# Seven block products for eight in the gate and up projections of a streaming encoder step on one Trainium2 core

## The chip, the cores and the metric

The kernel runs on one core of a Trainium2 chip. A core has a matrix engine (TensorE, in profiles PE, with its weight loads as PEld), a vector engine (DVE), an activation engine (ACT), a general engine (POOL, also GpSimd) and a queue engine (SP) that here issues the loads and stores. Tiles lie in SBUF on up to 128 partitions; matrix products accumulate in the banks of a second memory, PSUM. The metric is the device time of one execution in microseconds. Before the change it is 2217.21 us, the median of three runs from 2211.37 to 2221.53.

## The reference

One layer of a streaming encoder is applied to 1024 prompt frames and to 32 sample frames, with D_MODEL = 1024 and D_FF = 2816, all in fp32:

```python
def adaln_in(x, g, shift, scale):
    return rmsnorm(x, g) * (1 + scale[:, None, :]) + shift[:, None, :]

def swiglu(h, w_gate, w_up, w_down):
    return (jax.nn.silu(h @ w_gate) * (h @ w_up)) @ w_down

    mod = jax.nn.silu(c) @ w_mod + b_mod
    sh1, sc1, g1, sh2, sc2, g2, sh3, sc3, g3 = jnp.split(mod, N_MOD, axis=-1)
    h = adaln_in(x, gains[0], sh1, sc1)
    x = x + FFN_RES * g1[:, None] * rmsnorm(swiglu(h, w1_gate, w1_up, w1_down), gains[1])
    ...  # attention in two head groups, out-projection, residual with g2
    h = adaln_in(x, gains[4], sh3, sc3)
    x = x + FFN_RES * g3[:, None] * rmsnorm(swiglu(h, w2_gate, w2_up, w2_down), gains[5])
```

So two feed-forward networks (FFNs) stand around an attention part. The modulation is the product of SiLU(c) with a 1024 x 9216 matrix, for two vectors c (prompt and sample). The outputs are the new frames and the newest rows of keys and values.

## The kernel before

Activations lie transposed, features on partitions and tokens along the free dimension, in three token blocks: block 0 and block 1 of 384 tokens, block 2 of 288 (256 prompt frames and the 32 sample frames). A normed input `h` of a block is kept as two fp32r tiles, `h_hi` (the rounded value) and `h_lo` (the rest). A weight is loaded as fp32 (`raw`) and split in the same way: ACT copies it rounded into `w[:, 0]`, and DVE subtracts that from the raw tile into `w[:, 1]` (`split_w`, L299 to L305). A product of one 128-row k-tile is then three matmuls, high by high, high by low and low by high (`mm3`, L324 to L327).

An FFN (`ffn`, L525 on) goes over 11 groups of two hidden tiles of 128 columns. For each block and hidden tile, `up` makes the gate and the up product over 8 k-tiles in two PSUM banks, ACT applies SiLU, DVE multiplies, and the result is split into `gg`. `down` multiplies two hidden tiles into the 8 output tiles, two at a time in a two-bank tile `dn`, and DVE adds that to the accumulator `facc` (L581). The downs of a block are put one `up` behind (`late`). `rounds` gives the order of groups and blocks: in the first FFN ("h1") all blocks together, but the last three groups first for blocks 0 and 1 and then for block 2, and in the second ("h3") the first two groups for blocks 0 and 1 and then for block 2.

Other work runs beside the FFN as generators in the list `side`: `step(n)` takes n yields from the first of them. An `up` takes two steps after each of its two products (`PACE`), ten in the first group (`FAST`), and `down` one for each `dn`. In the first FFN these are the norms of the next blocks, and after the first group the modulation's remaining columns (`mod_aside`, L215 to L242: 14 chunks of 512 columns, made on DVE by multiplying raw rows with a per-partition scalar and adding, then transposed and reduced), and then the bias rows of attention. The first four chunks of the modulation are made on PE before the FFN starts (`mod_chunk`, L175), in the order of `START`. `need(key)` runs the side work until a key is done, `finish` until nothing is left. `between` makes a block's residual and its next norm; `finale` makes the output.

The order on each engine is chosen by a planner at build time: of the instructions that are ready by its own clock it takes the one that comes first in the program, and a tile is given a buffer when one of its pool is free. Pools live for the whole kernel: `wpool` (8 split weights), `rpool` (3 raw tiles), `gpool`, `hpool` (5 buffers) and `spool`; `upool` holds the large activation tiles. PSUM has two double banks (`p2`), three single ones (`p1`) and one more (`pc`). All loads go through SP's queue, in order.

## Time and profile before

| | |
|---|---|
| median of three runs | 2217.21 us (2211.37 to 2221.53) |
| profiled execution: span from first to last instruction | 2215.8 us; the page gives no other time for this execution |
| mean granted TensorE clock | 0.984 of full speed |
| busy PE, DVE, ACT, POOL | 2161.6, 1239.1, 697.8, 179.2 us |
| PE waits, longest in total | first input load 7.8 us; DVE's `ry` 4.8 us; POOL's `sq` 4.0 us |
| read from HBM, written | 164.12 MB, 22.86 MB |

A row of a group of instructions gives the line of the kernel, the engine and the operation, output and inputs by their names with partitions and elements, and the count; then the busy time and the mean of one in ns; then the idle time of the engine just before them and what ended it. A row of the timeline gives start, duration and the instruction. Matmuls overlap: the next starts before the one before it has ended, so the distance between two starts is the price of one, and the mean of one is not. A row of windows gives a stretch, its length, the busy time of PE, weight loads, DVE, ACT and POOL with the number of instructions, the granted clock, the DMA engines' share and GB/s; where only one tile is asked for, engines that do not touch it are left out.

### The profile page before, as it was taken

The page shows a single profiled execution, that of the slowest core. Times are in us where ns is not written, and L with a number is a line of the kernel's source. Part 1 is how long each engine was busy: PE and PEld are TensorE (multiplying, and loading weights), DVE is VectorE, ACT ScalarE, POOL GpSimd, SP SyncE. Part 2 cuts the span into 40 slices and gives each one's busy share as a digit, 9 for nine tenths or more (in the row PEclk, how much of TensorE's full clock was granted, in tenths as well). Part 3 has the DMA queues.
Part 4 walks back from the last instruction along what each step waited for, and adds up shares of the span by engine and source line. Part 5 has one row for each costly group of instructions (what it writes and reads, how often), then busy time and mean ns, then how long its engine had stood idle before and what let it go on. Part 6 is the DMA issues. An engine that isn't in the chain of part 4 may idle for free.

```text
span 2215.8 us, 33976 instructions
## 1 busy us (share of the span) xinstructions
PE 2161.6 (98%) x14012; PEld 2068.6 (93%) x14012; DVE 1239.1 (56%) x2425; ACT 697.8 (31%) x1450; POOL 179.2 (8%) x281
## 2 busy tenths in 40 slices
PE   6999999999999999899999899999999999999998
PEld 4999999999999999799787589999999999999998
DVE  5788667874333497677444865785333333333336
ACT  4411111111121253576444663542111111111133
POOL 1100000000000023001110313220000000000000
PEclk8999999999999999899999899999999999999999
DMA  9253334434122352111112121424211111111122
GB/s 323 93 153 118 111 96 124 143 101 129 39 66 69 101 184 93 38 39 30 50 30 62 46 77 67 134 86 120 66 58 39 57 39 39 58 38 58 39 69 79
DMA packets 200623, 186.03 MB, mean 84 GB/s; under 512 B 7597, under 2 KB 169813, under 8 KB 199317
## 3 DMA queue, kind: packets, MB, share of 16 engines
q1 hardware_dynamic: 200468, 183.87, 27.1%
q8 instruction: 110, 1.80, 0.3%
q14 instruction: 45, 0.36, 0.1%
HBM read 164.12 MB, written 22.86 MB: 84 GB/s over the span
## 4 chain that ended last, share of the span: by engine, by line
PE 90%; DVE 4%; DMA 3%; ACT 1%; issue 1%; POOL 0%; SPq 0%; ACTq 0%; DVEq 0%; POOLq 0%
PE dn L325 7%; PE dn L326 7%; PE dn L327 7%; PE gate L327 7%; PE gate L326 7%; PE up L327 7%; PE up L326 7%; PE gate L325 7%; PE up L325 7%; PE po L713 3%; PE S L752 2%; PE pq L325 2%; PE pq L327 2%; PE pq L326 2%; DMA raw<-in_w_gate_dram 1%; PE pp L776 1%
## 5 line engine op out<-in xcount | busy, mean ns | idle before, releaser
L326 PE MATMUL gate<-h_lo,w 128*128 128x384 f32 (+1 forms) x1056 | 340.2, 322 | 4.0 <-DVE h_lo L446 4.0
L325 PE MATMUL dn<-gg,w 128*128 128x384 f32 (+1 forms) x1056 | 341.4, 325 | 1.1 <-DVE facc L581 1.0
L581 DVE TENSOR_TENSOR facc<-dn,facc 128x768 f32<-128x768 f32 (+1 forms) x240 | 212.9, 889 | 230.2 <-PE dn L327 229.9
L326 PE MATMUL dn<-gg,w 128*128 128x384 f32 (+1 forms) x1056 | 340.6, 323 | 0.6 <-DVE gg L554 0.6
L325 PE MATMUL gate<-h_hi,w 128*128 128x384 f32 (+1 forms) x1056 | 341.0, 323 | 0.0
L327 PE MATMUL gate<-h_hi,w 128*128 128x384 f32 (+1 forms) x1056 | 340.4, 322 | 0.0
L325 PE MATMUL up<-h_hi,w 128*128 128x384 f32 (+1 forms) x1056 | 340.2, 322 | 0.0
L326 PE MATMUL up<-h_lo,w 128*128 128x384 f32 (+1 forms) x1056 | 340.0, 322 | 0.0
L327 PE MATMUL dn<-gg,w 128*128 128x384 f32 (+1 forms) x1056 | 340.0, 322 | 0.0
L327 PE MATMUL up<-h_hi,w 128*128 128x384 f32 (+1 forms) x1056 | 339.9, 322 | 0.0
L304 DVE TENSOR_TENSOR w<-raw,w 128x1024 fp32r<-128x1024 f32 x187 | 231.5, 1246 | 150.5 <-ACT w L303 150.3
L303 ACT ACTIVATE w<-raw 128x1024 fp32r<-128x1024 f32 x187 | 195.7, 1056 | 266.1 <-PE dn L327 103.5
L550 ACT ACTIVATE sl<-gate 128x384 f32<-128x384 f32 (+1 forms) x132 | 60.9, 462 | 563.9 <-PE gate L327 560.9
L551 DVE TENSOR_TENSOR sl<-sl,up 128x384 f32<-128x384 f32 (+1 forms) x132 | 68.5, 519 | 292.1 <-PE up L327 286.1
L326 PEld LDWEIGHTS gate<-h_lo,w 128*128 128x128 f32 x1056 | 198.6, 188 | 4.6 <-DVE h_lo L446 4.6
L325 PEld LDWEIGHTS dn<-gg,w 128*128 128x128 f32 x1056 | 199.2, 189 | 1.6 <-DVE facc L581 1.2
L326 PEld LDWEIGHTS dn<-gg,w 128*128 128x128 f32 x1056 | 199.2, 189 | 1.0 <-DVE gg L554 0.9
L327 PEld LDWEIGHTS dn<-gg,w 128*128 128x128 f32 x1056 | 199.1, 189 | 0.0
L325 PEld LDWEIGHTS gate<-h_hi,w 128*128 128x128 f32 x1056 | 198.7, 188 | 0.1
L327 PEld LDWEIGHTS gate<-h_hi,w 128*128 128x128 f32 x1056 | 198.7, 188 | 0.0
L327 PEld LDWEIGHTS up<-h_hi,w 128*128 128x128 f32 x1056 | 198.7, 188 | 0.0
L325 PEld LDWEIGHTS up<-h_hi,w 128*128 128x128 f32 x1056 | 198.5, 188 | 0.0
(224 smaller groups left out, 3367.4 us busy)
## 6 DMA issues: line engine op xcount, KB each, us to landing
raw<-in_w_mod_dram SPq DMA_DIRECT2D x56, 512.0 KB, 4.0
raw<-in_w_gate_dram SPq DMA_DIRECT2D x54, 512.0 KB, 4.0
raw<-in_w_up_dram SPq DMA_DIRECT2D x54, 512.0 KB, 4.7
raw<-in_w_down_dram SPq DMA_DIRECT2D x54, 512.0 KB, 4.5
raw<-in_w_in_dram SPq DMA_DIRECT2D x18, 512.0 KB, 4.3
wm<-in_w_mod_dram SPq DMA_DIRECT2D x8, 1024.0 KB, 7.4
raw<-in_w_out_dram SPq DMA_DIRECT2D x13, 512.0 KB, 4.5
xr<-xs SPq DMA_DIRECT2D x16, 384.0 KB, 3.5
```

Of the source, the lines that this page charges most:

```text
L303: ae.activation(w[:, 0], r, AF.Copy)
L304: ve.tensor_sub(w[:, 1], r, w[:, 0])
L325: te.matmul(ps, w[:, 0, k], hi, start=start, stop=False)
L326: te.matmul(ps, w[:, 0, k], lo, start=False, stop=False)
L327: te.matmul(ps, w[:, 1, k], hi, start=False, stop=stop)
L550: ae.activation(sl[:, :w], ps[0][:, :w], AF.Silu)
L551: ve.tensor_tensor(sl[:, :w], sl[:, :w], ps[1][:, :w], op=OP.mult)
L581: ve.tensor_tensor(o, ps[:, :, :w], o, op=OP.add)
L713: te.matmul(po[64 * h:64 * h + 64, :n], vsl(j, h, kn), PT(h, j, kn), start=j == 0, stop=j == nt - 1)
L752: te.matmul(S[:, c:ce], self.T[:, h, :], KQ[:, 0, 128 * k0 + c:128 * k0 + ce], start=True, stop=True)
L776: te.transpose(pp[:, j - j0, :], P[:, 128 * j:128 * j + 128], ident)
```

## The change

For each group, the gate and the up matrix are taken as 2 x 2 blocks: two hidden tiles (f) by two halves of the 1024 features (d), A11, A12, A21, A22, each four k-tiles of 128 columns. The inputs of blocks 0 and 1 are the 2 x 2 blocks on the other side: B11 and B21 are the halves of block 0, B12 and B22 those of block 1. Seven products (the Winograd form of Strassen's scheme) take the place of eight. Four weight sums S1 to S4 are made on POOL from raw quarters for each matrix of a group and then split like the other quarters; four input combinations T1 to T4 are made once per FFN (`combos`) from `h_hi + h_lo`, with half of the sums of high and low on POOL, and split again. The products are accumulated in PSUM where two follow on one another in the same bank (S2 and S3 in b, S1 and S4 in d, A11 and A12 in a), and DVE adds banks to SBUF tiles ("plus", five times a stage). Block 2 is multiplied by the plain quarters A11, A12, A22, A21 within the same stage. The first group of each FFN, and rounds that have only block 2, remain plain (`plain`), by quarters.

Gate, up and down of a group are now stages one after another, each for all its blocks; in a down stage the blocks come in the order 1, 0, 2. A stage's raw weights are loaded at the start of the stage before it, and its first sums or splits are made before that one ends (`ready`). A raw tile holds half of the features by two hidden tiles (1 KB rows) in place of all of them by one (512 B rows); the bytes are the same. Split weights are quarter tiles of 512 elements. `step(PACE)` is taken after each product of a Strassen stage, eight to a stage, or seven without block 2.

The modulation beside the FFN takes 384 columns at a time in 19 chunks, its raw rows in `hpool`, and yields ten times in a chunk, where it yielded 15 times. The pools of raw tiles, split weights, `gg` and small tiles, and a new one of large tiles `ux`, are opened anew for each of the three phases (`open_pools`), in the same addresses; an instruction on a new tile waits for the tiles that lay there before. At the start a modulation chunk is loaded by three transfers in place of two, and both hidden tiles' gate weights of the first group are loaded where the first hidden tile's gate and up were.

The core of the diff:

```diff
-ROUNDS = {"h1": ((), 3), "h3": ((((0, 1), 2), ((2,), 2)), 0)}
+ROUNDS = {"h1": (0, 3), "h3": (2, 0)}
+FFN1 = {"ux": 3, "r": 4, "w": 4, "g": 6, "s": 11}
+FFN2 = {"ux": 3, "r": 5, "w": 4, "g": 6, "s": 9}
+MIX = {"w": 8, "r": 3, "g": 5, "s": 5, "m": 1}
+MODS = [(("ux", 6), ("r", 2))] * 4
+SUMS_POOL = ("S1", "S2", "S3", "S4")
+ZPOOL = (1, 0, 1, 0)
+LATE = 1
...
+    def open_pools(name, **sizes):
+
+        phase.close()
+        pools.clear()
+        for tag, bufs in sizes.items():
+            pools[tag] = phase.enter_context(tc.tile_pool(name=name + tag, bufs=bufs, reuse_waits="tile"))
...
+    def mod_aside(c0, nc_):
+
+        w = 128 * nc_
+        acc = [s_tile([128, 384], "macc")[:, :w] for _ in range(2)]
         for g in range(4):
-            r = rpool.tile([128, 2, 512], F32, name="raw", tag="r")
-            dma.dma_start(r, w_mod[0, 256 * g:256 * (g + 1), 512 * n:512 * (n + 1)]
...
-            yield
-            yield
-            yield
+                yield
...
+    def mod_all(first):
+        for c0 in range(first, 72, 3):
+            yield from mod_aside(c0, min(3, 72 - c0))
...
+    def pair_of(src, tag="w", at=None):
+
+        w = at if at is not None else t_tile(tag, [128, 2, 4, 128], "w", F32R)
+        ae.activation(w[:, 0], src, AF.Copy)
+        ve.tensor_tensor(w[:, 1], src, w[:, 0], op=OP.subtract)
+        return w[:, 0], w[:, 1]
...
+        def of(self, name):
+            a = self.a
+            if name not in a:
+                x, y, op = {"S1": ("A21", "A22", OP.add), "S2": ("S1", "A11", OP.subtract),
+                            "S3": ("A11", "A21", OP.subtract), "S4": ("A12", "S2", OP.subtract)}[name]
+                x, y = self.of(x), self.of(y)
+                a[name] = h_tile([128, 4, 128], "ws")
+                (ge if name in SUMS_POOL else ve).tensor_tensor(a[name], x, y, op=op)
+            return a[name]
+
+        def split(self, name):
+            if name not in self.done:
+                self.done[name] = pair_of(self.of(name), *(self.places.pop(0) if self.places else ()))
+            return self.done[name]
+
...
+    def product(ps, w, x, first, last):
+        n = len(x[0])
+        for k in range(n):
+            for q, (a, b) in enumerate(((0, 0), (0, 1), (1, 0))):
+                te.matmul(ps, w[a][:, k, :], x[b][k], start=first and k == 0 and q == 0,
+                          stop=last and k == n - 1 and q == 2, skip_group_check=True)
...
+            def cut(name, v):
+                o = t[name]
+                ae.activation(o[:, 0, s, :], v, AF.Copy)
+                ve.tensor_tensor(o[:, 1, s, :], v, o[:, 0, s, :], op=OP.subtract)
+
+            ve.tensor_tensor(z[1, 1], z[1, 1], z[1, 0], op=OP.subtract)
+            yield
+            cut("T3", z[1, 1])
+            ve.tensor_tensor(z[1, 0], z[1, 0], z[0, 0], op=OP.subtract)
+            yield
+            cut("T1", z[1, 0])
+            ve.tensor_tensor(z[0, 0], z[0, 0], z[1, 1], op=OP.add)
+            yield
+            cut("T2", z[0, 0])
+            ve.tensor_tensor(z[0, 1], z[0, 1], z[0, 0], op=OP.subtract)
+            yield
+            cut("T4", z[0, 1])
+            yield
...
+    def rounds(key):
+        lead, lag = ROUNDS[key]
+        both, n, out = (0, 1, 2), NF // 2, []
+        if lead:
+            out += [(g, (0, 1)) for g in range(lead)] + [(g, (2,)) for g in range(lead)]
+        out += [(g, both) for g in range(lead, n - lag)]
+        out += [(g, (0, 1)) for g in range(n - lag, n)] + [(g, (2,)) for g in range(n - lag, n)]
         return out
 
-    def ffn(key, H, F, wg, wu, wd, per_group, key_out, after, beside=lambda ff, tb: None):
-        late, pre = [], {}
-        plan = rounds(*ROUNDS[key])
+    STRASSEN = [("A11", "B11", "a", 2), ("S2", "T2", "b", 0), ("S1", "T1", "d", 0), ("S3", "T3", "b", 0),
+                ("A22", "T4", "e", 2), ("S4", "B22", "d", 0), ("A12", "B21", "a", 2), ("A21", None, None, 2)]
+
...
+        def strassen(r, what, m, two, beside):
+            w, w2 = 384, TB[2][1]
+            B = {"B11": half(0, 0), "B21": half(0, 1), "B22": half(1, 1), **T}
+            banks, v = {}, {}
...
+            seq = [x for x in STRASSEN if two or x[1]]
+            for n, (name, x, at, blk2) in enumerate(seq):
+                w_ = m.split(name)
+                if n + 1 < len(seq):
+                    m.split(seq[n + 1][0])
+                if x:
+                    product(bank(at), w_, B[x], name in ("A11", "S2", "S1", "A22"), True)
+                if two and blk2:
+                    f, d = int(name[1]) - 1, int(name[2]) - 1
+                    product(bank(str(f)), w_, half(2, d), name in ("A11", "A22"), True)
+                beside(n)
+                if name == "A11":
+                    ae.activation(temp("s", 1, 0), banks["a"], AF.Copy)
+                elif name == "S2":
+                    plus(temp("u", 0, 1), "b", "s")
+                elif name == "S3":
+                    plus(v["s"], "b", "s")
+                    plus(temp("c", 1, 1), "d", "s")
+                    made(r, what, 1, 1, v["c"])
+                elif name == "A22":
+                    plus(v["s"], "e", "s")
+                    made(r, what, 1, 0, v["s"])
+                elif name == "S4":
+                    plus(v["u"], "d", "u")
+                    made(r, what, 0, 1, v["u"])
+                elif name == "A12":
+                    made(r, what, 0, 0, banks["a"])
+                    if two:
+                        made(r, what, 0, 2, banks["0"])
+                elif name == "A21":
+                    made(r, what, 1, 2, banks["1"])
+                step(PACE)
+
...
+            if what == "d":
+                for q in range(2):
+                    m.split(q, 0)
+                order = [tb for tb in (1, 0, 2) if tb in blocks]
+                ending = any(r == final[tb] for tb in order)
+                todo = [(tb, mp) for tb in order for mp in range(4)] if ending else \
+                    [(tb, mp) for h in range(2) for tb in order for mp in (2 * h, 2 * h + 1)]
+                for n, (tb, mp) in enumerate(todo):
+                    if n == 1:
+                        for q in range(2):
+                            m.split(q, 1)
+                    down(r, tb, m, mp)
+                    nexts(n, len(todo) - 3)
+            elif r == 0:
...
+                strassen(r, what, m, 2 in blocks, lambda n: nexts(n, 4 if what == "g" else 5))
...
-            begin("mod", mod_all(4, 18))
+            begin("mod", mod_all(16))
...
+    open_pools("mx", **MIX)
...
+    open_pools("f2", **FFN2)
```

More of the change, by code (lines that the diff above doesn't have):

```diff
@@ L100, in g_tile @@
     def g_tile(shape, name, dt=F32):
[L101 removed]
+        return t_tile("g", shape, name, dt)
     def h_tile(shape, name, dt=F32):
@@ L606, in ffn, with load @@
-        late.pop()()
+        T, sl, gs, loaded = {}, {}, {}, {}
+        stages = []
+        for r, (gi, blocks) in enumerate(plan):
+            held = [stages.pop()] if r and blocks == plan[r - 1][1] == (2,) else []
+            stages += [(r, "g"), *held, (r, "u"), (r, "d")]
+        def load(i):
+            if i >= len(stages) or stages[i] in loaded:
+                return
+            r, what = stages[i]
+            gi, blocks = plan[r]
+            if what == "d":
+                loaded[r, what] = Rows(wd, gi, "ux" if key == "h1" and blocks == (2,) else "w")
+            else:
+                loaded[r, what] = Mat((wg, wu)[what == "u"], gi)
@@ new lines, in ready, with made @@
+        def ready(i):
+            if i >= len(stages):
+                return
+            load(i)
+            r, what = stages[i]
+            m = loaded[r, what]
+            if what == "d":
+                m.split(0, 0)
+                m.split(1, 0)
+            elif r and plan[r][1] != (2,):
+                m.of("S4")
+            else:
+                m.split("A11")
+        def made(r, what, f, tb, src):
+            w = TB[tb][1]
+            if what == "g":
+                if (r, f, tb) not in sl:
+                    sl[r, f, tb] = s_tile([128, 384], "sl")[:, :w]
+                ae.activation(sl[r, f, tb], src, AF.Silu)
+                return
+            v = sl[r, f, tb]
+            g = gs[r, f, tb] = g_tile([128, 2, 384], "gg", F32R)
+            ve.tensor_tensor(v, v, src, op=OP.mult)
+            ae.activation(g[:, 0, :w], v, AF.Copy)
+            ve.tensor_tensor(g[:, 1, :w], v, g[:, 0, :w], op=OP.subtract)
@@ new lines, in half, with plain @@
+        def half(tb, d):
+            return [e[4 * d:4 * d + 4] for e in H[tb][:2]]
+        def plain(r, what, m, tb, beside):
+            w = TB[tb][1]
+            names = [f"A{f + 1}{d + 1}" for f in range(2) for d in range(2)]
+            for n, name in enumerate(names):
+                f, d = divmod(n, 2)
+                if d == 0:
+                    ps = p1("gate" if what == "g" else "up")
+                w_ = m.split(name)
+                if n < 3:
+                    m.split(names[n + 1])
+                product(ps[:, :w], w_, half(tb, d), d == 0, d == 1)
+                beside(n)
+                if d == 1:
+                    step(FAST if r == 0 else PACE)
+                    made(r, what, f, tb, ps[:, :w])
```

377 lines of the change are left out of this document (222 added, 155 removed).

## The prediction

> **What bounds the kernel now.** I read first the page's busy shares, its chain of waits and the windows of long stretches.
>
> ```profile
> span 2215.8 us, 33976 instructions
> PE 2161.6 (98%) x14012; PEld 2068.6 (93%) x14012; DVE 1239.1 (56%) x2425; ACT 697.8 (31%) x1450; POOL 179.2 (8%) x281
> PE 90%; DVE 4%; DMA 3%; ACT 1%; issue 1%; POOL 0%; SPq 0%; ACTq 0%; DVEq 0%; POOLq 0%
> 110.00:770.00 660.00, 660.00 (x4122) 659.28 (x4121) 394.30 (x611) 119.76 (x180) 3.04 (x3) 1.00 0.35 103
> 1719.00:1788.00 69.00, 69.00 (x434) 69.00 (x433) 23.82 (x30) 11.47 (x18) 0.00 (x0) 1.00 0.15 46
> ```
>
> TensorE sets the time. The window columns are stretch and length, then busy time of PE, weight loads, DVE, ACT and POOL, granted clock, DMA share and GB/s. From 110 to 770 us, the first FFN, PE never idles. The second row is one steady group of two hidden tiles of the second FFN: 69.0 us, DVE 23.82 us of it. Busy time overlaps between matmuls, so a matmul's price is the distance between starts:
>
> ```profile
> 1701.96 0.33 PE L325 MATMUL up<-h_hi,w 128*128 128x384 f32 x1
> ...
> 1706.12 0.29 PE L325 MATMUL dn<-gg,w 128*128 128x288 f32 x1
> ...
> 1709.28 0.33 PE L325 MATMUL gate<-h_hi,w 128*128 128x384 f32 x1
> ```
>
> 24 matmuls of 384 columns take 4.16 us, 0.1733 each; 24 of 288 columns take 3.16 us, 0.1317 each. A group has 288 of the first and 144 of the second: 49.9 + 19.0 = 68.9 us, the window's 69.0. So the FFNs run at the pace of issue, and a matmul left out is worth its 0.1733 us as long as nothing else becomes late.
>
> **The change, part by part.**
>
> *Matmuls removed.* For one matrix and one group the two 384-token blocks took 2 x 2 x 2 products of 4 k-tiles x 3 passes, 96 matmuls; seven products take 84. Block 2 keeps its 48 of 288. The first group of each FFN and the rounds with block 2 alone stay plain, so in each FFN 10 rounds x 2 matrices are Strassen stages: 40 stages x 12 = 480 matmuls, 480 x 0.1733 = **-83.2 us**. A group falls from 68.9 to 64.7 us.
>
> *Vector work added.* The prices:
>
> ```profile
> L304 DVE TENSOR_TENSOR w<-raw,w 128x1024 fp32r<-128x1024 f32 x187 | 231.5, 1246 | 150.5 <-ACT w L303 150.3
> L551 DVE TENSOR_TENSOR sl<-sl,up 128x384 f32<-128x384 f32 x88 | 48.7, 553 | 270.0 <-PE up L327 264.1 <-issue 5.7
> L581 DVE TENSOR_TENSOR facc<-dn,facc 128x768 f32<-128x768 f32 x160 | 152.7, 956 | 172.3 <-PE dn L327 172.0
> L420 DVE SCALAR_TENSOR_TENSOR n<-xt,acoef,pr 128x384 f32<-128x384 f32 x8 | 4.3, 610 | 0.1
> ```
>
> Between 384 and 1024 elements a two-input operation grows by 693 ns / 640 = 1.083 ns an element, so a 512-element quarter split costs 0.553 + 0.139 = 0.69 us. Per group: 16 quarter splits for gate and up, 11.1 us, where four whole ones took 5.0; the down splits +0.3; ten block sums from PSUM (five "plus" a stage) 5.5. That is +11.9 us, 35.7 us of DVE in 64.7. In the second FFN that is 55% and hidden. In the first FFN the modulation product shares DVE:
>
> ```profile
> 110.00:165.00 55.00, 55.00 (x343) 54.94 (x342) 46.19 (x70) 9.68 (x15) 0.00 (x0) 1.00 0.51 154
> 110.00:550.00 440.00, 16.76 (x112) 13.93 (x112) 148.87 (x224) 1.00 0.41 121
> L227 DVE TENSOR_SCALAR macc<-raw,csil 128x512 f32<-128x512 f32 x28 | 12.9, 483 | 7.2 <-DMA raw<-in_w_mod_dram 7.2
> L229 DVE SCALAR_TENSOR_TENSOR macc<-raw,csil,macc 128x512 f32<-128x512 f32 x196 | 137.8, 749 | 15.4 <-DMA raw<-in_w_mod_dram 15.1
> L240 DVE TENSOR_REDUCE modT<-pmt 128x4 f32<-128x512 f32 x28 | 19.2, 685 | 4.1 <-PE pmt L239 4.1
> ```
>
> (The second row is the stretch of the accumulator alone, without the ACT and POOL columns.) The same 56 column tiles now go in 19 chunks of 384 columns. A chunk is 14 accumulations at 0.61 (L420's shape), two starts at 0.483 - 0.139 = 0.34 and two reductions at 0.55: 10.3 us in 10 yields, about 1.03 us a step. A Strassen round takes 16 + 16 + 12 = 44 steps, so the 190 steps, 12 of them beside round 0's downs, fall into 178 / 44 = 4.05 rounds at 45 us of DVE each; before, 210 steps at 36 a group spread over 5.8. In these four rounds DVE is asked for 35.7 + 45 = 81 us in 64.7.
>
> Does PE pay? Bounds: nothing, if the modulation falls back into the idle DVE time of rounds 5 to 10, since its coefficients for the residual are wanted only at the FFN's end; 4.05 x (81 + 5 of POOL contention, below - 64.7) = 86 us, if DVE keeps program order strictly. For the whole FFN the demand is 394 + 7 x 11.9 + 3 x 10.5 (rounds without block 2: two quarters fewer) + 3 x 0.9 (the lagging rounds) + 16 (the modulation's smaller pieces) = 527 us of 660 - 42 = 618, 85%. The first row above shows DVE at 46.19 of 55, 84%, with PE idle for nothing. That is near the zero end; I take **+15**, because the load comes in front and not evenly.
>
> *Loads.* Weights come in as many loads of as many bytes as before; the modulation issues 76 in place of 56, and its first four chunks 12 in place of 8:
>
> ```profile
> 1409.24 0.38 SPq L301 DMA_DIRECT2D raw<-in_w_up_dram  x1
> ```
>
> 24 x 0.38 = 9 us more of SP's issue time over some 300 us; with DMA at 0.35 of its time in the first FFN this costs nothing. The modulation's tiles now share the five h buffers with the block sums, of which S4's is held for a stage; that slows the modulation, which is the good case of the bounds above.
>
> *Weight sums on POOL.* Four of 512 elements a stage.
>
> ```profile
> L368 POOL TENSOR_TENSOR sq<-sq 128x384 f32<-128x384 f32 x32 | 35.3, 1116 | 1422.0 <-ACT sq L364 1400.0 <-PE S L752 13.3 <-DVE w L304 5.0
> L467 POOL TENSOR_TENSOR facc<-facc,xr 128x768 f32<-128x768 f32 x4 | 7.3, 1852 | 39.5 <-DVE facc L464 39.5
> 1423.22 3.40 DVE L467 TENSOR_TENSOR fo<-fo,xr 128x768 f32<-128x768 f32 x2
> 1421.28 3.65 POOL L467 TENSOR_TENSOR fo<-fo,xr 128x768 f32<-128x768 f32 x2 [13.63 <-DVE fo L464]
> ```
>
> Between the first two rows 512 elements cost 1.36 us; eight a group, 10.9 of 64.7 us on an engine that stood idle. But beside POOL's two adds the DVE adds of the same shape take 1.70 us each against 0.956 in L581's row: some 0.65 us lost for each POOL sum, 5 us a group, already in the bound above. [...]
>
> *Chains inside a stage.* Each product needs its split one product (2.08 us) ahead, and bank b or d read before the next product adds to it, again one product of cover. The chain is ACT 0.52, DVE 0.69 or 0.55:
>
> ```profile
> L303 ACT ACTIVATE w<-raw 128x1024 fp32r<-128x1024 f32 x187 | 195.7, 1056 | 266.1 <-PE dn L327 103.5 <-PE up L327 91.1 <-DMA raw<-in_w_gate_dram 39.8
> L553 ACT ACTIVATE gg<-sl 128x384 fp32r<-128x384 f32 x88 | 46.0, 522 | 317.2 <-DVE sl L551 317.2
> ```
>
> A 512-element ACT copy, by these, takes 0.63 us, so a split is 1.3 us after its sum. It fits; what is queued on DVE (a 0.96 us add to facc) can make it late. Where a round has no block 2 (four rounds), the last hidden block needs 0.55 + 0.55 + 0.52 + 0.55 = 2.2 us against 2.08 of cover. Bounds: 0 and half a microsecond a stage (20 us); I take **+6**.
>
> *Combinations T1 to T4.* 20 DVE operations of 768 elements, 19 us, once per FFN, between the second block's first product and round 1: 96 + 96 matmuls, 33 us of cover, shared with the adds to facc and the next block's norm. Bounds 0 and 8 each; **+4** for both.
>
> *Start and memory by phase.* The first gate matmul comes at 45.55 us behind the modulation's loads:
>
> ```profile
> 40.74 3.59 PE L186 MATMUL pm<-wm,csil 128*32 128x512 f32 x12 [2.46 <-DMA wm<-in_w_mod_dram]
> ...
> 45.55 0.42 PE L325 MATMUL gate<-h_hi,w 128*128 128x384 f32 x1
> raw<-in_w_gate_dram SPq DMA_DIRECT2D x54, 512.0 KB, 4.0
> ```
>
> Two 512 KB loads now stand where the first gate matrix needed one; **+2**, between 0 and 4.0. At the two phase changes the first weights wait on SP until a tile of the old phase at their address is released, with all later loads behind them: 4.0 + 1.06 + 1.25 = 6.3 us at most each, hidden where block 2's last rounds still run; **+4** for both. A long gap costs more than itself:
>
> ```profile
> 888.24 1.75 PE L405 MATMUL pr<-ident,ry 128*128 128x128 f32 x6 [2.44 <-DVE ry L338]
> 890.00:896.00 6.00, 2.98 (x13) 2.52 (x14) 5.94 (x21) 5.39 (x17) 0.56 (x1) 0.50 0.00 0
> ```
>
> After that wait the granted clock is 0.50 for six microseconds.
>
> *End.* The last downs now stand together, so two finales share DVE with block 2's. Bounds 0 and 8; **+2**:
>
> ```profile
> 2198.41 1.41 DVE L581 TENSOR_TENSOR facc<-dn,facc 128x576 f32<-128x576 f32 x2
> ...
> 2208.36 4.47 DVE L1315 SCALAR_TENSOR_TENSOR xp<-py,ry,xp 128x512 f32<-128x512 f32 x6
> ```
>
> *Sum.* -83.2 + 15 + 6 + 4 + 2 + 4 + 2 = -50.2; 2215.8 - 50.2 = 2165.6 us of span. The page gives only the span; the median of the runs is 1.4 us above it, so **2167 us**. Its own range, from the bounds, is 2145 to 2190.
>
> **The rivals.**
>
> *DVE takes over in the first FFN (slower).* One mechanism: the modulation's operations precede the later stages' splits and sums in DVE's order, so PE waits in rounds 1 to 4. Price 86 in place of 15: 2167 + 71 = 2238 us. It decides from the point where such a round takes 81 us: 64.7 + (83.2 - 18) / 4.05. For it: just that is asked of DVE there, before any contention. Against it: the coefficients are not urgent, and DVE at 84% cost PE nothing. Chance 0.13.
>
> *Chains exposed in every stage.* 40 stages x 1 us of waits in place of 6: 2167 + 34 = 2201 us. For it: 2.1 us of cover where the old kernel's gate and up could wait a whole 4.2 us pair; against it: a DVE half idle in the second FFN. Chance 0.17, with half a DVE backlog (2167 + 28 = 2195) giving about the same.
>
> *Nothing is lost.* All covers hold: 2217 - 83 + 5 = 2139 us. For it: no PE wait at all from 110 to 770 now. Chance 0.16.
>
> *It does not do what it says.* If the round plan left stages plain, each pair of them would give 4.2 us back; half of them would leave 2217 - 42 + 33 = 2208. The loops show 40 stages; chance 0.04.
>
> **How the numbers follow.** The forecast has 0.50. Changes under 0.5% (11 us; the runs themselves spread from 2211 to 2222) can't be told from none. Faster than 2206: the forecast, "nothing lost" and most of the exposed chains, 0.50 + 0.16 + 0.13 = 0.79. Within: 0.09, the rest of these and a partial backlog. Slower: 0.12. The range 2130 to 2222 leaves out most of the slower rival and a little below.
>
> **What would show it.** Right: 480 fewer gate and up matmuls of 384 columns; 64.7 us groups in the second FFN with PE never idle, DVE near 36 us in each; the modulation still running past the fourth round. Wrong: PE waits on DVE's splits or sums before 400 us, with DVE above 95% there; waits of PE on splits in every stage of the second FFN; granted clock at 0.5 at a phase change.

## The result: slower, by 164 us

The changed kernel takes 2381.12 us (2377.4 to 2381.55) against 2217.18 us for the kernel before on the same chip: a ratio of 1.0743, 95% interval 1.072 to 1.0765. The forecast was 2167, its range ended at 2222. The page after, first its span, busy shares and chain:

```profile
span 2379.7 us, 34693 instructions
PE 2158.8 (91%) x13532; PEld 2036.6 (86%) x13532; DVE 1583.0 (67%) x3077; ACT 849.1 (36%) x1814; POOL 440.5 (19%) x449
PE 72%; DVE 19%; issue 3%; DMA 3%; ACT 1%; POOL 1%; SPq 0%; DVEq 0%; ACTq 0%; POOLq 0%
```

The 480 matmuls are gone (14012 to 13532), and yet PE is busy as long as before (2158.8 us, 2161.6 before): it waits, and it runs at a lower clock. PE is idle for 221 us of its span, where it was for 54, and the 83 us of matmuls left out came back almost whole in its busy time, while the mean granted clock fell from 0.984 to 0.945. PE's part of the chain fell from 90% to 72%, DVE's rose from 4% to 19%. The next rows are windows of the changed kernel (columns as in the prediction): the first FFN where the modulation runs, then one steady round of the second FFN.

```profile
110.00:495.00 385.00, 332.01 (x1952) 320.60 (x1951) 360.10 (x665) 83.53 (x151) 63.73 (x41) 0.93 0.38 113
1831.00:1902.00 71.00, 67.94 (x409) 66.78 (x409) 38.28 (x54) 18.05 (x35) 12.20 (x8) 0.96 0.15 45
```

In the first, DVE is busy 94% of the time and PE 86%. In the second, DVE is busy for only 38.3 of 71 us, near the predicted 35.7, and the round still takes 71 us, not 64.7. So two things went wrong, and only one of them looks like a full DVE.

The times by stretch, in us, from the trace: "FFN" is from its first gate matmul to the start of its last `dn`, "between" from there to the other FFN's first gate matmul. "Period" is from the first `dn` of a group to the first of the next. Kernels below the second line are the experiments that follow.

```text
kernel           FFN 1   between  FFN 2   periods 1-5 of FFN 1           first of FFN 2   steady in FFN 2
before           804.0   564.6    784.4   about 71.4 (3 x 23.8)          -                69.0
changed          873.8   597.2    847.0   87.9 85.7 83.9 84.3 76.7       97.0             70-71.2
eight            831.3   590.6    795.6   74.6 75.3 81.5 75.7 76.2       59.9             69.0
mod_2            880.4   595.4    850.5   82.2 81.9 77.6 76.7 80.7       96.9             70-71.9
s4_last          854.7   587.4    793.1   86.3 79.8 86.9 76.8 78.1       86.9             65.1
s4_nomod         824.6   588.6    793.4   80.1 73.5 74.5 73.8 73.7       86.4             65.1
h1_eight_mod2    801.4   586.7    793.5   70.4 70.4 71.0 70.4 71.0       86.3             65.1
late_t           800.8   586.6    768.5   70.4 70.4 71.0 70.4 71.0       57.5             65.1
```

**What a stage end looks like.** PE's waits in the second FFN of the changed kernel (engine, line, releaser, total us, times, longest), and then the end of one up stage in time order:

```profile
PE dn L795 <- ACT gg L696: 12.5, 10, 3.2
PE g L597 <- DVE sl L695: 9.7, 8, 1.2
PE g L597 <- DVE w L540: 5.8, 8, 0.7
PE dn L796 <- DVE gg L697: 1.7, 3, 1.4
```
```profile
1890.41 0.51 PE L597 MATMUL ge<-h,w 128*128 128x384 f32 x2
...
1891.71 1.79 POOL L563 TENSOR_TENSOR ws<-raw 128x512 f32<-128x512 f32 x1 [28.85 <-DMA raw<-in_w_gate_dram]
1892.27 1.64 DVE L695 TENSOR_TENSOR sl<-sl,ut 128x384 f32<-128x384 f32 x1
...
1894.11 2.25 PE L597 MATMUL gu<-h,w 128*128 128x384 f32 x12
...
1896.98 0.44 DVE L695 TENSOR_TENSOR sl<-sl,g 128x288 f32<-128x288 f32 x1
1897.35 1.39 DVE L540 TENSOR_TENSOR w<-raw,w 128x512 fp32r<-128x512 f32 x1
1897.57 0.37 PE L597 MATMUL g<-h_hi,w 128*128 128x288 f32 x1 [1.21 <-DVE sl L695]
1897.78 0.29 PE L597 MATMUL g<-h_lo,w 128*128 128x288 f32 x1
...
1898.79 0.53 PE L597 MATMUL g<-h_hi,w 128*128 128x288 f32 x2 [0.72 <-DVE w L540]
...
1900.37 0.44 PE L597 MATMUL g<-h_hi,w 128*128 128x288 f32 x1
...
1900.85 0.63 ACT L539 ACTIVATE w<-raw 128x512 fp32r<-128x512 f32 x1 [3.82 <-PE g L597]
...
1901.38 1.59 ACT L696 ACTIVATE gg<-sl 128x384 fp32r<-128x384 f32 x4
...
1901.94 1.01 PE L795 MATMUL dn<-gg,w 128*128 128x384 f32 x2 [1.13 <-ACT gg L696]
```
```profile
1901.90:1906.40 4.50, 4.46 (x13) 4.18 (x14) 1.98 (x5) 1.07 (x3) 1.27 (x1) 0.50 0.75 240
2044.40:2048.90 4.50, 4.34 (x23) 4.02 (x24) 2.87 (x6) 1.01 (x3) 0.78 (x1) 1.00 0.76 262
```

The last product of the stage, A21 for block 2 (`g`), starts late because DVE has not yet read the other half of its bank pair, pauses for the second half of A21's split, and then the first `dn` waits for the `gg` of block 1, whose work came out of S4. These are the three operations PE finds unfinished at eight up stage ends one after another. PE does not follow the program here: the planner put S4's product (`gu<-h`, from 1894.11) behind A12's (`ge<-h`, from 1890.41), so that only A21 for block 2 covers what follows S4. The last 0.6 us of the third wait is ACT's order, in which a split of the next weights (from 1900.85) stands ahead of that `gg`.

The first of the two windows shows the price that no wait lists: a granted clock of 0.50 for 4.5 us, `dn` matmuls 0.32 us apart instead of 0.17. The second stands behind the same three waits two rounds on, where the granted clock stayed at 1.00; half clock followed at six of the eight ends. The waits, 3.1 us a round (1.21, 0.72 and 1.13), and some 2.2 us for half clock at those six (an estimate, half of the 4.5 us at 0.50) make up most of the 6 us.

### The profile page after: what moved, and what is told of

It reads as the page before. It is cut to its first block, busy times and chain, and to the rows that moved or that the text cites. A ratio compares the mean times of both kernels' runs of the same rounds, so it can differ in the third digit from the quotient of the medians.

```text
span 2379.7 us, 34693 instructions
## 1 busy us (share of the span) xinstructions
PE 2158.8 (91%) x13532; PEld 2036.6 (86%) x13532; DVE 1583.0 (67%) x3077; ACT 849.1 (36%) x1814; POOL 440.5 (19%) x449
## 4 chain that ended last, share of the span: by engine, by line
PE 72%; DVE 19%; issue 3%; DMA 3%; ACT 1%; POOL 1%; SPq 0%; DVEq 0%; ACTq 0%; POOLq 0%
PE gu L597 11%; PE ge L597 8%; PE dn L795 6%; PE g L597 6%; PE dn L796 6%; PE dn L797 6%; DVE macc L250 4%; DVE w L540 3%; PE gate L597 3%; PE po L978 2%; PE S L1017 2%; PE pq L342 2%; DVE sl L695 2%; PE pq L344 2%; PE pq L343 2%
## 5 line engine op out<-in xcount | busy, mean ns | idle before, releaser
L539 ACT ACTIVATE w<-raw 128x512 fp32r<-128x512 f32 x298 | 186.1, 630 | 615.7 <-PE dn L797 226.4
L540 DVE TENSOR_TENSOR w<-raw,w 128x512 fp32r<-128x512 f32 x298 | 220.9, 745 | 161.3 <-ACT w L539 160.4
L597 PE MATMUL gu<-t,w 128*128 128x384 f32 x1440 | 264.7, 335 | 0.0
L597 PEld LDWEIGHTS gu<-t,w 128*128 128x128 f32 x1440 | 248.6, 188 | 0.3 <-issue 0.2
L597 PE MATMUL g<-h_hi,w 128*128 128x288 f32 x1024 | 232.2, 300 | 18.1 <-DVE sl L695 9.7
L597 PEld LDWEIGHTS g<-h_hi,w 128*128 128x128 f32 x1024 | 175.9, 191 | 23.3 <-ACT w L539 12.0
L597 PE MATMUL ge<-h,w 128*128 128x384 f32 x960 | 194.4, 337 | 1.3 <-DVE w L540 0.9
L597 PEld LDWEIGHTS ge<-h,w 128*128 128x128 f32 x960 | 167.4, 188 | 1.9 <-DVE w L540 1.3
L250 DVE SCALAR_TENSOR_TENSOR macc<-wma,csil,macc 128x384 f32<-128x384 f32 (+1 forms) x266 | 165.1, 661 | 1.0 <-DMA wma<-in_w_mod_dram 1.0
L597 PE MATMUL g<-h_lo,w 128*128 128x288 f32 x512 | 152.5, 298 | 0.0
```

The source lines that it names most:

```text
L250: ve.scalar_tensor_tensor(acc[j], r[:, kk], c, acc[j], op0=OP.mult, op1=OP.add)
L539: ae.activation(w[:, 0], src, AF.Copy)
L540: ve.tensor_tensor(w[:, 1], src, w[:, 0], op=OP.subtract)
L597: te.matmul(ps, w[a][:, k, :], x[b][k], start=first and k == 0 and q == 0, stop=last and k == n - 1 and q == 2, skip_group_check=True)
```

## The experiments

Theories at the start: (A) the modulation in front overloads DVE in the first FFN; (B) POOL's sums hold DVE at the stage ends; (C) the start of the second FFN waits for a tile that the combinations read; (D), the rival to all, the stages, quarter tiles and memory by phase lose the time, and not Strassen. Times are medians against the changed kernel's 2381, ratios against the kernel before. The runs were on several chips, on which the kernel before took 2213.8 to 2217.2 us, so a difference of 3 us between two kernels says nothing.

**Sums on DVE.**

```diff
-SUMS_POOL = ("S1", "S2", "S3", "S4")
+SUMS_POOL = ()
```


> Edit: the four block sums of a stage (S1 to S4) run on DVE, none on POOL; all else as in the changed kernel. Theory 'POOL's sums hold DVE': at the end of each up stage POOL's sums of the next stage stretch DVE's operations with two inputs in memory from 0.55 to 1.64 us; without them a round of the second FFN falls from 70 to 65 to 66 us, and the kernel gets 30 to 60 us shorter although DVE has 8 x 0.69 = 5.5 us more to do in a round. Rival 'DVE has too much to do': rounds of the second FFN stay at 70 us or more, the first five of the first FFN grow by 5.5 us each, and the kernel gets some 25 us longer.

Measured: 2369.09 us, ratio 1.0691 (1.067 to 1.0712). Steady rounds stay at 70 to 71 us. Two rows of DVE in the second FFN, first of the changed kernel, then with the sums on DVE (both from 1650 to 2250 us):

```profile
L695 DVE TENSOR_TENSOR sl<-sl,ut 128x384 f32<-128x384 f32 x26 | 24.4, 938 | 0.0
```
```profile
L695 DVE TENSOR_TENSOR sl<-sl,ut 128x384 f32<-128x384 f32 x24 | 13.2, 549 | 0.0
```

The contention is real (0.94 against 0.55 us), and moving the sums gains 12 us in all. The stage end above shows one case: POOL's first sum ends at 1893.50 us, the `sl` that began beside it at 1893.91. Theory B falls as the main cause, and so does "too much to do", though in this run less contention and 5.5 us more DVE work a round could cancel in part. The new order below settles it: it keeps the sums on POOL and their contention, and a round takes 65.1 us.

**Thinner modulation.**

```diff
                         ve.scalar_tensor_tensor(acc[j], r[:, kk], c, acc[j], op0=OP.mult, op1=OP.add)
                 yield
+                yield
```


> Edit: the modulation product gives way twice after each pair of accumulations, not once, so that it spreads over about 342 / 44 = 7.8 rounds in place of 4.1. Theory 'the modulation in front holds PE': rounds 1 to 5 of the first FFN fall from 84 to about 70 us, later ones grow to about 70 from 67, DVE falls below 52 of 55 us in the stretches before 495 us; 50 to 60 us shorter in all, the rest of the kernel unchanged. Rival 'the accumulations only fill gaps that PE's stages leave anyway': the work per round stays and total time changes by less than 15 us.

Measured: 2389.94 us, ratio 1.0801 (1.0776 to 1.0825). A stretch of it:

```profile
385.00:440.00 55.00, 47.36 (x277) 46.18 (x276) 45.71 (x84) 14.71 (x28) 7.61 (x5) 0.91 0.41 123
```

The early rounds get shorter, but now seven of the first eight stay between 76 and 82 us: the sum over the eight is 624 us, in the changed kernel it is 614. With DVE at 83% PE still waits. So a saturated DVE is not the cause by itself; beside these chains an accumulation costs PE time at 94% and at 83%.

**Combinations earlier.**

```diff
-                    step(FAST if r == 0 else PACE)
+                    step(FAST if r == 0 and (key == "h1" or tb) else PACE)
```


> Edit: in the first group of the second FFN the side work gets 2 steps in place of 10 after each half of the first block's products, so that the combinations T1 to T4 come before block 2's residual and norm in program order. Theory 'the first down of block 1 waits for a tile that the combinations still read, and these stand behind block 2's norm': PE's wait of 26 us at 1577 us falls below 6 us, the kernel gets 15 to 25 us shorter. Rival 'the same work is only waited for later': block 2's norm comes later instead and its first products wait; within 8 us of the changed kernel.

Measured: 2378.07 us, ratio 1.0737 (1.0719 to 1.0755). The first period of the second FFN fell from 97.0 to 83.0 us: the waits for `facc` (29.4 us) are gone, and within it the first Strassen products (`gu`) now wait 8.2 us for ACT's split and 3.2 us for DVE's. The second FFN as a whole is 6 us shorter, and it begins 5 us later, which isn't explained. The rival was right on the total; that the same work is only waited for elsewhere explains a part.

**Eight products in the same stages.** A branch `eight` takes the place of `strassen`: A11, A12, A21, A22, each for blocks 0, 1 and 2, and each result read straight from its bank.

> Edit: same stages, quarter tiles, pools and order of the downs, but the two 384-token blocks take the eight plain products in place of seven: no block sums, no combinations T, no additions between banks, 480 matmuls (83 us) more. Theory 'Strassen's extra work on DVE and POOL costs what was lost': the second FFN returns to 69 us a round and the time to about 2381 - 215 + 83 = 2249 us, with the 33 us lost between the FFNs left over and up to 25 us from the modulation in front (DVE 30 + 45 = 75 us asked of 69). Rival 'the stages with quarter tiles and the memory by phase are the loss': PE waits at stage ends stay, rounds of the second FFN take 74 us or more, and the time is 2330 to 2464 us.

Measured: 2279.96 us, ratio 1.029 (1.0273 to 1.0307). With 480 matmuls more it is 101 us faster than the changed kernel. Its steady rounds are at 69.0 us, those of before. D falls for the rounds: the stage layout costs a steady round nothing. It keeps 26 us more between the FFNs, 27 in the first and 11 in the second: some 63 us of the loss are there without the seven products.

**Another order of the products.** My new theory after these: a stage's last products have too little cover. S4 goes to the end, A21 forward, and the downs start with the block whose results are oldest (the two edits weren't separated):

```diff
-                ("A22", "T4", "e", 2), ("S4", "B22", "d", 0), ("A12", "B21", "a", 2), ("A21", None, None, 2)]
+                ("A21", None, None, 2), ("A22", "T4", "e", 2), ("A12", "B21", "a", 2), ("S4", "B22", "d", 0)]
...
-                order = [tb for tb in (1, 0, 2) if tb in blocks]
+                order = [tb for tb in (0, 1, 2) if tb in blocks]
```


> Edit: another order of the products in a Strassen stage (A11, S2, S1, S3, A21 of block 2 alone, A22, A12, S4 in place of A11, S2, S1, S3, A22, S4, A12, A21), and the downs take block 0 first, then 1, then 2. Theory 'what follows a stage's last products has too little cover': A21's 1.6 us and A12's 2.1 us stand before downs that need results of S4 and A12, while these go through four operations on DVE and ACT; with block 0's downs between (4.2 us) and block 2's results early, rounds of the second FFN fall from 70.5 to 65 to 66 us, rounds without block 2 from 54 to about 48, and the kernel gets 50 to 75 us shorter. Rival 'DVE and ACT have too much to do around a stage end, in whatever order': rounds stay above 69 us, less than 20 us gained.

Measured: 2298.05 us, ratio 1.0371 (1.0351 to 1.0391): 83 us gained, half of the loss (54 in the second FFN, 19 in the first, 10 between them). All of PE's waits from 1650 to 2270 us, and a steady round:

```profile
PE dn L796 <- DVE gg L697: 1.7, 1, 1.7
PE dn L795 <- ACT gg L696: 1.0, 1, 1.0
```
```profile
1800.00:1865.00 65.00, 64.95 (x408) 64.42 (x407) 37.43 (x54) 18.52 (x34) 11.70 (x8) 1.00 0.16 49
L695 DVE TENSOR_TENSOR sl<-sl,ut 128x384 f32<-128x384 f32 x27 | 23.7, 879 | 0.6
```

The round is 65.1 us, against 64.7 predicted, with the same DVE work and the same stretched operations beside POOL (0.88 us): covered, they cost nothing.

**Modulation left out, or moved.** `elif k == 1` in place of `else` for the accumulations, which leaves out six of the eight k-tiles; or, in the second, a scaled copy on ACT and an addition on POOL for each of them; the third joins that to the new order.

> Edit: the modulation beside the first FFN accumulates only 2 of its 8 k-tiles (the products of the other 6 are left out, their loads stay), so 228 fewer operations of 384 columns on DVE. Theory 'an accumulation in DVE's queue delays what PE waits for, however thinly they are spread' (spread over twice the rounds they cost the same): rounds 1 to 5 of the first FFN fall to 66 to 70 us, 65 to 90 us shorter in all. Rival 'something else in the first FFN, such as the quarter splits themselves, sets these rounds': less than 40 us gained.

Measured: 2338.53 us, ratio 1.055 (1.0526 to 1.0574): 43 us gained, the theory's 65 missed. Rounds 1 to 5 fell to 71 to 80 us.

> Edit: each accumulation of the modulation becomes a scaled copy on ACT and an addition on POOL in place of one operation on DVE. Theory 'DVE's queue': with DVE free of the 304 operations rounds 1 to 5 of the first FFN fall to about 70 us, 50 to 85 us shorter. Rival 'POOL's additions hold DVE as much as DVE's own accumulations did': rounds 1 to 5 stay above 78 us, less than 30 us gained; second rival 'ACT's splits wait behind the 304 copies of about 0.5 us': rounds stay above 78 us with waits on ACT.

Measured: 2412.61 us, ratio 1.0893 (1.086 to 1.0927), slower than the changed kernel. PE's waits from 110 to 650 us, three of the four longest in total (the first is `dn` for `facc`, 18.6 us):

```profile
PE gu L599 <- DVE ut L744: 14.5, 4, 6.7
PE dn L797 <- ACT gg L698: 12.1, 5, 4.7
PE pmt L258 <- POOL macc L252: 8.9, 6, 5.7
```

ACT stands in the same chains as DVE, and PE's transposes (`pmt`) wait in their place in PE's order for POOL's sums (8.9 us in six waits). The copies also take buffers of the small tiles; their part isn't separated.

> Edit: the other product order with block 0's downs first, and the modulation on ACT and POOL, together. Theory 'two separate losses': the gains of the two alone add up to within 15 us, 100 to 150 us in all, some 2240 to 2280 us. Rival 'one and the same loss (DVE's queue at stage ends)': together they gain less than three quarters of the sum.

Measured: 2339.15 us, ratio 1.0568 (1.0526 to 1.061). Against the new order's 2298 the move costs 41 us, against the old order's 2381 it cost 31.

**With the new order: combinations earlier, modulation thinner, left out; mixer's memory.** The edits are those above on top of the new order; for the mixer, its raw tiles lie first in its memory and the first FFN's last down weights use `w`:

```diff
-MIX = {"w": 8, "r": 3, "g": 5, "s": 5, "m": 1}
+MIX = {"r": 3, "w": 8, "g": 5, "s": 5, "m": 1}
...
-Rows(wd, gi, "ux" if key == "h1" and blocks == (2,) else "w")
+Rows(wd, gi, "w")
```


> Edit: the other product order with block 0's downs first (2298 us), and in the second FFN's first group 2 side steps in place of 10 after each half of block 0's products. Theory 'the combinations stand behind block 2's residual and norm on DVE': with the stage ends mended, PE's wait of 20.5 us for the first copies to facc falls below 8 us and the kernel gets 12 to 20 us shorter than 2298. Rival 'block 2's norm is only waited for later, and the combinations' own 25 us of DVE work is the floor': within 6 us of 2298.

Measured: 2297.96 us, ratio 1.0369 (1.0351 to 1.0388): nothing. PE's longest waits from 1484 to 1650 us, without the edit and with it:

```profile
PE dn L795 <- DVE facc L800: 20.5, 1, 20.5
```
```profile
PE gu L597 <- ACT w L539: 8.2, 1, 8.2
PE dn L795 <- DVE facc L800: 8.0, 1, 8.0
PE pss L374 <- POOL sq L387: 6.9, 1, 6.9
```

The wait for `facc` shrank, and others took its place.

> Edit: the other product order with block 0's downs first, and the modulation gives way twice after each pair of accumulations. Theory 'a step puts up to four accumulations (2.4 us) ahead of a split that has 2.1 us of cover; thinner, 1.2 us fit into the slack that the new order leaves': 20 to 45 us shorter than 2298, rounds 1 to 8 at 70 to 74 us. Rival 'each accumulation costs PE the same wherever it stands' (as it did under the old order): within 10 us of 2298.

Measured: 2292.3 us, ratio 1.0349 (1.0333 to 1.0366): 6 us. The rival.

> Edit: the other product order with block 0's downs first, and the modulation accumulates 2 of its 8 k-tiles only (the other products left out). Under the old order leaving them out gained 43 us. Theory 'the two losses are separate': 2298 - 43 = 2255 us within 8 us. Rival 'a stage end that no longer waits exposes the accumulations elsewhere in the stage (rounds 1 to 5 still take 77 to 87 us)': 60 to 75 us gained, 2223 to 2238 us, with rounds 1 to 5 at 66 to 69 us. Either way, what is above the second FFN's 65 us in these rounds is not the modulation's.

Measured: 2263.77 us, ratio 1.0216 (1.0193 to 1.0239): 34 us, near the first theory. Round 1 still takes 80 us and rounds 2 to 5 take 74, with a quarter of the accumulations.

> Edit: the other product order with block 0's downs first; the mixer's raw tiles lie first in its memory, over tiles that hold T's, and the last down weights of the first FFN no longer use those tiles. Theory 'the mixer's first weights wait for memory that the first FFN's last rounds still use': PE's 8 us of waits for the first split weights at 900 us go, 7 to 14 us shorter than 2298. Rival 'the loads or the splits themselves are late, whatever lies below': within 4 us of 2298.

Measured: 2297.96 us, ratio 1.0369 (1.035 to 1.0387): nothing. The stretch between the FFNs fell from 587.4 to 573.6 us, and the first FFN grew from 854.7 to 872.6, its last `dn` waiting up to 5.8 us for DVE's `gg`. The mixer's earlier loads and splits had only changed places with the last rounds' work.

**A tile of its own for the modulation's loads.** With rounds of 74 us unexplained, I suspected the shared tiles and SP's queue:

```diff
-FFN1 = {"ux": 3, "r": 4, "w": 4, "g": 6, "s": 11}
+FFN1 = {"ux": 3, "r": 4, "w": 4, "g": 6, "s": 10, "q": 1}
...
-            r = h_tile([128, 2, 384], "wma")[:, :, :w]
+            r = t_tile("q", [128, 2, 384], "wma")[:, :, :w]
```


> Edit: product order with block 0's downs first (2298 us), and the modulation's weights come into one tile of their own, not into the five that the block sums use (one small tile less for gate and up results, 10 in place of 11). Theory 'the block sums and the weights' loads wait behind the modulation's loads': rounds 1 to 5 of the first FFN fall from 82 to 75 us or less, 25 us or more shorter than 2298. Rival 'the operations in DVE's queue alone set these rounds': within 10 us of 2292 to 2298 (a single tile also spreads the accumulations thinner, which alone gained 6 us).

Measured: 2419.86 us, ratio 1.0928 (1.0901 to 1.0954), 122 us longer; neither theory had that. PE's longest wait from 110 to 650 us, and SP's:

```profile
PE pmt L256 <- DVE macc L250: 88.2, 10, 19.5
```
```profile
SPq L241 <- DVE macc L250: 190.8, 63, 10.8
SPq L241 <- DMA wma<-in_w_mod_dram: 171.9, 67, 3.8
```

One buffer makes load and accumulation take turns. The modulation then runs later than the program order assumes, and PE reaches its transposes before the sums are there: 88 us of waits on the side work itself.

> Edit: as the one with a tile of their own for the modulation's weights, and 6 of the 8 k-tiles' products left out. Theory 'loads and shared tiles': rounds 1 to 5 fall from 74 to 66 to 69 us, 25 to 40 us shorter than 2264. Rival 'transposes, reductions, splits and ends of stages on DVE do it': rounds stay at 72 us or more, within 10 us of 2264.

Measured: 2294.13 us, ratio 1.0351 (1.0326 to 1.0376), 30 us slower than 2264. The single buffer spoils this test: it doesn't say what the shared tiles cost.

**Eight in the first FFN, seven in the second.**

```diff
-                strassen(r, what, m, 2 in blocks, ...)
+                (strassen if key == "h3" else eight)(r, what, m, 2 in blocks, ...)
```


> Edit: eight plain products in the first FFN, the seven in their other order in the second (240 matmuls more than with seven in both, 41.6 us). Theory 'in the first FFN the seven lose more than they save': the first FFN takes about 831 us in place of 855, the whole about 2274 us. Rival 'the order of the downs and of the products had already mended the first FFN, its rest is the modulation's in any form': the 41.6 us come on top, 2310 to 2340 us.

Measured: 2260.54 us, ratio 1.0201 (1.018 to 1.0223): 38 us shorter than 2298 with 41.6 us of matmuls more. In the first FFN the seven lose about 79 us before they save 41.6.

> Edit: as the one with eight products in the first FFN, and the modulation gives way twice after each pair of accumulations. Theory 'without Strassen's chains thinner accumulations hide': rounds 1 to 5 of the first FFN near 70 us, 10 to 25 us shorter than with eight alone, 2250 to 2264 us; still not below 2217, since the stretch between the FFNs is some 25 us longer in every form of the changed kernel. Rival 'each accumulation costs the same': within 6 us of eight alone.

Measured: 2244.69 us, ratio 1.0128 (1.0107 to 1.0149), 16 us shorter still. From 110 to 650 us PE waits for nothing, and rounds take 70.4 to 71 us, as before (71.4). Thinner accumulations, worth 6 us beside the seven and nothing in the old order, hide fully beside the eight.

**Late combinations, and raw tiles that outlive the phases.** The second round with blocks 0 and 1 in the second FFN is plain too, `combos` begins after it, and T4 is written last (its place is the half of block 1 that no product reads any more). The second kernel adds one pool of four raw tiles for all phases.

> Edit: eight products in the first FFN with the modulation thinner, the seven in their other order in the second (2245 us), and there the second round with blocks 0 and 1 takes eight products too (24 matmuls, 4.2 us, more), so that the combinations T1 to T4 are made after it, beside the rounds of block 2 alone. Theory 'the combinations at the start hold the first downs': the wait of 20.9 us goes, the second FFN's first period falls from 86 to 58 to 62 us, 18 to 28 us shorter, 2217 to 2227 us. Rival 'the start waits for block 2's residual and norm and for memory, the combinations only stand beside': less than 8 us gained.

Measured: 2219.94 us (2216.8 to 2224.48), ratio 1.002 (1.001 to 1.003): 25 us gained, the time of before to within 0.5%. The first period is 57.5 us. The three longest waits of PE from 1420 to 1560 us, and two windows, of the first FFN and of the phase change to the mixer:

```profile
PE gate L598 <- DVE w L541: 4.5, 1, 4.5
PE dn L824 <- DVE gg L703: 2.7, 1, 2.7
PE dn L823 <- DVE facc L828: 2.3, 2, 1.8
```
```profile
110.00:495.00 385.00, 385.00 (x2439) 384.31 (x2438) 253.01 (x462) 65.96 (x127) 0.00 (x0) 1.00 0.32 99
840.00:910.00 70.00, 58.15 (x425) 56.34 (x425) 49.48 (x116) 28.57 (x59) 20.19 (x16) 0.88 0.36 115
```

The wait of 20.5 us is gone: it was the combinations' place (in DVE's order or in memory, T4's tile moved too; the two aren't separated). The last row shows a part of what is left, PE idle 12 of 70 us behind the first FFN; before, from 845 to 915 us, it was 5.5. The two longest waits there (830 to 960 us) are for the mixer's first split weights:

```profile
PE pv L964 <- DVE w L338: 4.5, 1, 4.5
PE pv L963 <- ACT w L337: 3.1, 1, 3.1
```

> Edit: as the one with late combinations, and the raw weight tiles are four in memory of their own that lasts through all phases (4 in place of 4, 3 and 5; one small tile less in the mixer). Theory 'at a phase change the first weights wait for memory that the phase before still holds': the 8 us of waits at the mixer's first weights and the 4.8 us at the second FFN's go, 8 to 14 us shorter than late combinations alone. Rival 'the splits' own tiles are what waits' : within 4 us of late combinations alone.

Measured: 2242.07 us, ratio 1.0109 (1.0091 to 1.0126), 22 us worse than without. The mixer's first products still wait 5.6 us for a split, the second FFN's first gate still 1.5 us for DVE's split and 1.4 for ACT's, in place of 4.5 and 1.0, and with four raw tiles in place of five its rounds take 67 us:

```profile
PE g L600 <- DVE sl L703: 8.6, 6, 1.8
PE dn L825 <- DVE sl L703: 2.9, 3, 1.7
```

## Why the prediction was wrong, step by step

The forecast and the measurement are 214 us apart. The runs place them so:

```text
term of the sum          predicted   measured   from
chains inside a stage    +6          +83        2381 - 2298
DVE in the first FFN     +15         +95        2298 - 2245, and 41.6 of matmuls added
combinations T1-T4       +4          +29        2245 - 2220, and 4.2 of matmuls added (second FFN alone)
start, phases, end       +8          +40        2220 - (2217 - 37.4 for 216 matmuls fewer), all that remains
```

The measured sizes depend on the order in which the edits were put on: leaving out the same accumulations gained 43 us in the old order and 34 in the new.

*Matmuls removed: right.* 480 are gone, and a steady round with its waits taken away takes 65.1 us in place of 69.0, 3.9 of the predicted 4.2 us. DVE's work in a steady round was right as well (37.4 us of 65 against 35.7). All three signs of a wrong forecast came true in the main: PE waits before 400 us with DVE near saturation, waits in each round of the second FFN (not in each stage), and a granted clock of 0.50 behind the first FFN (from 920 to 947 us).

*Chains inside a stage: the step that failed first.* The prediction priced each chain by itself, 2.2 us against a cover of 2.08, half a microsecond a stage. It measured 2.1 us a stage on the mean (83 / 40); in the second FFN, where the waits are at the up stages' ends alone, 5 to 6 us a round. I had seen that "what is queued on DVE can make it late" and bounded it by a wait for one operation. But the results of A12, S4 and A21 end together, S4's with an addition, each with a product, a copy and a subtraction, beside the next stage's sums: from 1891 to 1902 us the additions, products and subtractions stand one behind the other on DVE, while the cover after S4, which PE ran after A12, is block 2's 1.6 us. DVE's 55% said nothing on that. And a wait was priced at its own length, where half clock added some 2.2 us to 3.1 at six ends of eight. My rival "chains exposed in every stage" had the mechanism at half its size, 1 us a stage, and in every stage; it didn't see that an order of the products, with that of the downs, settles it.

*DVE in the first FFN: the term was above its bound.* The rival's place, rounds 1 to 4, and its round of 86 us come close to the 84 to 88 measured, its size in part by luck: it too was priced by DVE's capacity. The step that failed is the choice near zero: I let the accumulations fall back into idle DVE time. Spread to 83% of DVE, they cost the same. The runs fit the rival's mechanism, that each accumulation stands in DVE's order ahead of splits with 2.1 us of cover, and that PE's transposes stand in PE's order; they don't prove it. Beside eight products the same work, spread thinner, hides fully. The 95 us are the seven's and the modulation's together, the first FFN's combinations included; leaving out three quarters of the accumulations gains only 34. What else holds those rounds at 74 us, the modulation's loads, its transposes or the shared tiles, stays open.

*POOL's sums: the slowdown is there, and it costs little.* By the two runs' DVE rows from 1650 to 2250 us it is some 0.48 us a sum (30.6 us in all, 64 sums), where I took 0.65; with the sums on DVE the kernel gains 12 us. I read the 1.70 us in the kernel before as what each addition took beside POOL, and that was wrong: it is the mean of one addition of 2.53 us, which ended 0.81 us after POOL's second, and one of 0.95 us that began later. In the changed kernel a DVE operation on two SBUF inputs that began beside a sum ended 0.41 to 0.55 us after it, in all 42 cases of seven rounds, six a round (the last section has more).

*Combinations: mis-sized.* 33 us of cover were counted. The prediction named the adds to `facc` and the next block's norm as sharing it and priced neither: on DVE block 2's residual and norm came first, then the combinations, and behind these the copies to `facc` that `dn` waited for. I priced the combinations' work and not their place.

*Start: the wrong way, but small* (-2.8 us for +2, whose bounds were 0 and 4.0). *End: right* (+1.9 for +2). *Phase changes: too small*, 22 us between the FFNs in the best variant against +4 for both. Some 8 us (4.5 + 3.1) are the mixer's first weights; two layouts of memory only moved them. The last row of the table holds another 21 us in the second FFN, where no term stood for them; PE still waits 17 us there, almost all before 1600 us. The rest isn't settled.

The rivals "nothing is lost" and "it does not do what it says" fall with the first rows.

## What to carry to other kernels

An engine that is half idle can still hold another (DVE was busy for 38.3 of 71 us in the second FFN): what decided here is the order of a burst at a stage end against the cover of the product behind it, so look at the last 10 us of a stage, not at a share. Before shortening a covered engine's work, list what its covers hide and let the last product of a stage be one whose result is needed last. Work that is not urgent can cost where it stands in an engine's order ahead of urgent work, and spreading it helped here only beside a longer cover: thinner accumulations gained nothing in the old order, 6 us in the new and 16 us beside the eight products.

## What the runs showed of the hardware

In the changed kernel short waits were followed by half clock at some stage ends and not at others. From 1896 to 1902 us PE had three waits of 1.21, 0.72 and 1.13 us with matmuls between (the rows of the stage end), and from 1899.8 to 1906.5 us the granted clock was 0.50, so only the first two waits lie before it. The same three waits came at eight stage ends of the second FFN, and at six of them half clock followed. At the other two it stayed at 1.00 (from 1757 to 1766 and from 2042 to 2049 us). No wait at these eight ends was longer than 1.21 us, and the two before the half clock are 1.9 us together.

The `sl` products of 128x384 on two SBUF inputs took up to 1.64 us beside a POOL sum, 0.94 on the mean of 26, against 0.55 with the sums on DVE. In the rounds from 1760 to 2255 us of the changed kernel all 42 DVE operations on two SBUF inputs that began while a sum ran (`sl`, `gg` and splits) ended 0.41 to 0.55 us after that sum, as if they had stood until it was through. The 28 block sums and products with one input in PSUM that began beside a sum kept their 0.44 to 0.56 us and ended before it.
